# Modulation tiles of the first feed-forward network: three buffers of their own instead of the weights' raw buffers

## The chip, the cores and the metric

The kernel is one program on one NeuronCore of a Trainium2 chip. Its time is the device time of one execution in microseconds (us). The engines are named as in the profile: PE (TensorE, matrix products), PEld (its weight loads), DVE (VectorE), ACT (ScalarE), POOL (GpSimd) and SP (SyncE, which issues nearly all transfers). Each engine works through its own instructions in a fixed order.

## The reference

Two layers of a hybrid block run over 512 latent tokens and 256 context tokens of width 1024. Each layer has a token mixer (a state-space scan with heads, differential attention and an S5 scan side by side) and a convolutional feed-forward network of width 2816. Before and after each of them stand RMS norms, and shifts, scales and gates ("modulation") that are computed from a conditioning vector. The lines of the reference that matter here:

```python
mod_l = (jax.nn.silu(c) @ mod_w[layer] + mod_b[layer])[:, None, :]
mod_c = jax.nn.silu(c_ctx) @ mod_w[layer] + mod_b[layer]
sh_a, sc_a, g_a, sh_f, sc_f, g_f = jnp.split(mod_l, N_MOD, axis=-1)
...
def conv_ffn(h, w_gate, w_up, conv_w, conv_b, w_down):
    g = dwconv(h @ w_gate, conv_w, conv_b)
    return (jax.nn.silu(g) * (h @ w_up)) @ w_down
```

All of it is in float32. mod_w of one layer is a matrix of 1024 x 6144; the kernel has it as 48 tiles of 128 x 1024 (six groups j of eight tiles). The second layer's last group of context values isn't needed.

## The kernel before

**Products in float32.** A weight tile (128 x 1024, 512 KB) is loaded into a buffer with the tag "raw" (load_split, L129 to L139). ACT rounds it to a high half `hi` (L138), DVE subtracts that from the raw tile and writes the low half `lo` (L139). PE then makes three products for each tile: hi by hi, hi by lo and lo by hi (mm3, L144 to L146). There are two raw buffers (`w_raw` = 2) and three pairs of hi and lo (`w_hl` = 3).

**The first feed-forward network** (ffn, L1223) stands in the first layer, over 512 latent columns (products into pl) and 256 context columns (into pc). For each of the 22 slices f of the width of 2816 it loads wg, projects, applies the convolution on ACT and DVE (L1257, L1261), the silu (L1262), loads wu, projects, multiplies (L1267), and splits the result into ahi and alo (L1270, L1271). For each two slices the down projection (out_group, L1189) loads two wd tiles, makes the products into ma and adds them to y in SBUF: by ACT copies for the first pair (L1215), by DVE additions for the others (L1217). That is 66 weights in the whole network.

**Work put in between.** After each half of a slice `between()` (L1515) takes one or two steps of a generator `mod` and some of a generator `setup`. `setup` prepares the S5 scan of the second layer: small operations on DVE (L373 to L525), tables s5x on POOL (L551 to L556 and L598 to L603), products of those on PE (L568, L569) and transposes (L575). `mod` (L339) computes the modulation values: in this network mod_rest (L1569) has 56 tiles of mod_w left, eight of the first layer (j = 5) and all 48 of the second. Each tile is loaded by SP (L348); DVE multiplies it by a row (silu of c, "crow") and sums (L351). Where the context needs a value too (nv == 2: the first 24 of the 56 tiles), POOL multiplies the tile by the second row in place (L355) and ACT sums it (L357). The other 32 tiles have only L351.

**What sets the order.** The Python code gives the order in which work is declared; a scheduler then simulates times and orders each engine's instructions by them. A tile may be loaded into a buffer only when all who read its last contents are done. A pool's tag with bufs=n is a ring of n such buffers. In the kernel before, the 56 tiles take their buffers from the weights' ring: `raw=True` makes them the tag "raw" of the pool `self.W`, with `w_raw` = 2. SP issues all these loads in one queue, so a load that waits for its buffer holds back those behind it.

Of the kernel before, what the change touches and what calls it, by code (L numbers as in the profile page):

```python
# [92 lines left out]
class Kern:  # L93
# [242 lines left out]
                nc.vector.tensor_mul(o, o, wb)  # L336
                self.gate_out(l, j, nv)

    def mod(self, l, js, pool, row, pool_share, raw=False, pin=False):  # L339


        nc = self.nc
        for j in js:
            nv = 2 if l < L - 1 or j < 2 else 1
            for i in range(8):
                m = j * 8 + i
                w = self.t(self.W, [128, 1024], "raw", bufs=self.w_raw) if raw else self.t(pool, [128, 1024], "modw", bufs=2)
                nc.sync.dma_start(w, self.I["modw"][l, m])  # L348
                o = self.modc[l][:, m]
                jk = self.t(pool, [128, 1024], "modj", BF16, bufs=1)  # L350
                ins = nc.vector.scalar_tensor_tensor(jk, w, 1.0, row[:, 0], op0=ALU.mult, op1=ALU.mult, accum_out=o[:, 0:1])  # L351
                if pin:
                    self.tc.keep_in_program_order(ins)
                if nv == 2 and pool_share(i):
                    nc.gpsimd.tensor_mul(w, w, row[:, 1])  # L355
                    junk = self.t(self.small, [128, 1024], "junk", BF16, bufs=1)
                    nc.scalar.activation(junk, w, AF.Copy, accum_out=o[:, 1:2])  # L357
                elif nv == 2:
                    jk = self.t(pool, [128, 1024], "modj", BF16, bufs=1)
                    nc.vector.scalar_tensor_tensor(jk, w, 1.0, row[:, 1], op0=ALU.mult, op1=ALU.mult, accum_out=o[:, 1:2])  # L360
                if i < 7:
                    yield
            o = self.modc[l][:, j * 8:(j + 1) * 8, :nv]
            nc.vector.tensor_add(o, o, self.modb[:, l, j * 8:(j + 1) * 8, None].to_broadcast([128, 8, nv]))
            self.mod_scale(l, j, nv)
            yield
# [914 lines left out]
    def run(self):  # L1281
        tc, nc, I = self.tc, self.nc, self.I
        from contextlib import ExitStack
        with ExitStack() as es:
# [54 lines left out]
            M = self.modc[0]  # L1339
            mod = self.mod_pe((1, 0), PA)  # L1340
            pump(mod, 2)
            self.s5_disc(0, P0)
            v, g = nc.vector, nc.gpsimd
            setup = self.s5_setup(0, P0, (g, v, g, v, g, v, g, v), 2, True)
            pump(mod, 4)
            for t, nme in ((cst, "cst"), (self.nw, "nw"), (self.modb, "modb")):
                nc.sync.dma_start(t, I[nme])
            pump(setup, SU0)
            xts = []
            for t in range(6):  # L1350
                if t < 3:
                    pump(mod, 1)
                xt = self.t(PA, [128, 1024], "xr", bufs=6)
                nc.sync.dma_start(xt, xin(t))
                xts.append(self.normalise(xt, xt))
# [212 lines left out]

    def mod_rest(self, pool):  # L1569
        row = self.silu_rows(pool)  # L1570
        yield from self.mod(0, (5,), pool, row, lambda i: True, True)
        yield from self.mod(1, range(6), pool, row, lambda i: True, True)

    def open(self, name, bufs, kw):

# [148 lines left out]
```

## Time and profile before

| | |
|---|---|
| median of three runs | 1914.52 us (1913.77 to 1920.86) |
| profiled execution, its own time | 1921.23 us |
| its span, mean granted clock of PE | 1919.5 us, 0.957 |
| PE busy | 1736.8 us (90%) |
| DVE busy | 1258.9 us (66%) |
| ACT busy | 737.6 us (38%) |
| POOL busy | 541.3 us (28%) |
| transfers | 254.39 MB, 133 GB/s in the mean |

The busy time of an engine is the sum over its instructions; register, branch, semaphore and transfer-issuing instructions don't count. The first feed-forward network lies between about 560 and 1160 us of the span, the second between about 1560 and 1880. A row of a timeline gives the start, the duration, the engine, the line and what it writes and reads, and in brackets how long the engine had been idle and what ended it. A row of waits gives who waited, for whom, how long in sum, how often and the longest one.

### The profile page before, as it was taken

How to read it: one execution, taken by the hardware profiler on the slowest of the kernel's cores; microseconds unless marked ns; L12 is line 12 of the kernel's file. 1: busy time of each engine (PE TensorE's matmuls, PEld its weight loads, DVE VectorE, ACT ScalarE, POOL GpSimd, SP SyncE). 2: the span in 40 equal slices, each digit the busy share in tenths (PEclk: the TensorE clock that was granted, in tenths of full speed). 3: DMA queues.
4: the chain of work that ended last, by engine and by line, in shares of the span. 5: the costliest groups of instructions: out<-in, count | busy, mean ns of one | idle time of the engine just before them, and what ended most of it. 6: DMA issues, size and time to landing. Idle time of an engine off the chain costs nothing.

```text
span 1919.5 us, 25989 instructions
## 1 busy us (share of the span) xinstructions
PE 1736.8 (90%) x9573; PEld 1474.9 (77%) x9573; DVE 1258.9 (66%) x2201; ACT 737.6 (38%) x1383; POOL 541.3 (28%) x669
## 2 busy tenths in 40 slices
PE   6999787886999899999999997997888989999998
PEld 1788676775788788888778886885778788888886
DVE  6888997776568455556556557669667464555555
ACT  2443223755444433322122235533555444232322
POOL 5446940020235554412500024098000210000002
PEclk8999887998999999999999998998999999999999
DMA  8364347364443334434533433433285343232322
GB/s 313 133 198 144 121 143 202 89 182 119 168 133 99 104 117 132 135 129 128 168 121 126 146 107 120 133 111 113 88 204 117 132 157 112 83 110 79 119 77 88
DMA packets 128814, 254.39 MB, mean 133 GB/s; under 512 B 42608, under 2 KB 65712, under 8 KB 128688
## 3 DMA queue, kind: packets, MB, share of 16 engines
q1 hardware_dynamic: 125312, 249.57, 41.9%
q10 hardware_dynamic: 3376, 3.17, 0.5%
q8 instruction: 75, 1.23, 0.3%
q14 instruction: 51, 0.42, 0.1%
HBM read 213.53 MB, written 41.16 MB: 133 GB/s over the span
## 4 chain that ended last, share of the span: by engine, by line
PE 47%; DMA 11%; DVE 10%; POOL 4%; ACT 4%; issue 4%; SPq 1%; POOLq 0%; DVEq 0%; ACTq 0%
DMA raw<-in_modw 4%; PE pl L146 4%; PE pl L144 4%; PE pl L145 4%; PE ma L144 3%; PE ma L145 3%; PE ma L146 3%; PE pc L145 3%; PE pc L146 3%; PE pc L144 3%; DVE lo L139 3%; PE pp L144 3%; PE pp L145 3%; PE pp L146 3%; PE ma L1153 2%
## 5 line engine op out<-in xcount | busy, mean ns | idle before, releaser
L139 DVE TENSOR_TENSOR lo<-raw,hi 128x1024 fp32r<-128x1024 f32 (+2 forms) x190 | 248.3, 1310 | 191.6 <-ACT hi L138 190.4
L138 ACT CAST hi<-raw 128x1024 fp32r<-128x1024 f32 (+2 forms) x190 | 197.3, 1042 | 444.7 <-PE pl L145 128.1
L176 POOL TENSOR_SCALAR rv<-ss 128x1 f32<-128x1 f32 x51 | 20.6, 404 | 760.2 <-ACT junk L184 751.0
L146 PE MATMUL pl<-Hl,lo 128*128 128x512 f32 (+1 forms) x560 | 215.8, 385 | 12.8 <-DVE lo L139 12.8
L144 PE MATMUL pl<-Hl,hi 128*128 128x512 f32 (+1 forms) x560 | 215.5, 385 | 5.5 <-DVE xt L245 5.0
L145 PE MATMUL pl<-Hl,hi 128*128 128x512 f32 (+1 forms) x560 | 214.0, 382 | 0.0
L1217 DVE TENSOR_TENSOR y<-y,ma 128x512 f32<-128x512 f32 x160 | 106.6, 683 | 86.9 <-PE ma L146 86.7
L144 PE MATMUL ma<-hi,ahi 128*128 128x512 f32 x360 | 141.3, 393 | 5.9 <-DVE y L1217 5.9
L145 PE MATMUL ma<-lo,ahi 128*128 128x512 f32 x360 | 140.7, 391 | 0.1
L146 PE MATMUL ma<-hi,alo 128*128 128x512 f32 x360 | 139.8, 389 | 0.0
L351 DVE SCALAR_TENSOR_TENSOR modj<-raw,crow 128x1024 bf16<-128x1024 f32 x56 | 71.4, 1275 | 97.9 <-DMA raw<-in_modw 95.1
L146 PEld LDWEIGHTS pl<-Hl,lo 128*128 128x128 f32 x560 | 107.6, 192 | 33.9 <-DVE lo L139 14.7
L144 PEld LDWEIGHTS pl<-Hl,hi 128*128 128x128 f32 x560 | 107.7, 192 | 24.6 <-issue 5.2
L145 PEld LDWEIGHTS pl<-Hl,hi 128*128 128x128 f32 x560 | 107.3, 192 | 18.6
L144 PE MATMUL pp<-Hl,hi 128*128 128x512 f32 (+1 forms) x256 | 99.7, 392 | 13.4 <-DVE y L1217 5.5
L146 PE MATMUL pp<-Hl,lo 128*128 128x512 f32 (+1 forms) x256 | 98.1, 384 | 2.8 <-DVE lo L139 2.8
L144 PE MATMUL pc<-Hc,hi 128*128 128x256 f32 x352 | 99.6, 284 | 0.7 <-DVE de L394 0.7
L145 PE MATMUL pc<-Hc,hi 128*128 128x256 f32 x352 | 100.0, 284 | 0.2 <-DVE Hc L216 0.2
L146 PE MATMUL pc<-Hc,lo 128*128 128x256 f32 x352 | 99.7, 284 | 0.0
L145 PE MATMUL pp<-Hl,hi 128*128 128x512 f32 (+1 forms) x256 | 99.2, 388 | 0.2
L144 PE MATMUL pp<-hi,Hl 128*128 128x256 f32 (+1 forms) x256 | 89.3, 353 | 6.4 <-DVE xt L249 4.8
L145 PE MATMUL pp<-lo,Hl 128*128 128x256 f32 (+1 forms) x256 | 88.9, 347 | 2.4 <-DVE lo L139 2.4
(489 smaller groups left out, 4647.3 us busy)
## 6 DMA issues: line engine op xcount, KB each, us to landing
raw<-in_modw SPq DMA_DIRECT2D x56, 512.0 KB
raw<-in_wg SPq DMA_DIRECT2D x44, 512.0 KB
raw<-in_wu SPq DMA_DIRECT2D x44, 512.0 KB
raw<-in_wd SPq DMA_DIRECT2D x44, 512.0 KB
raw<-in_winf SPq DMA_DIRECT2D x28, 512.0 KB
modw<-in_modw SPq DMA_DIRECT2D x24, 512.0 KB
modw<-in_modwn SPq DMA_DIRECT2D x16, 512.0 KB
raw<-in_wout SPq DMA_DIRECT2D x16, 512.0 KB
```

The lines of the kernel that those rows point to most:

```text
L138: nc.scalar.copy(hi[:, :cols], raw[:, :cols])
L139: (eng or nc.vector).tensor_sub(lo[:, :cols], raw[:, :cols], hi[:, :cols].bitcast(F32))
L144: mm(out, lhs[0], rhs[0], start=first, stop=False)
L145: mm(out, lhs[0], rhs[1], start=False, stop=False)
L146: mm(out, lhs[1], rhs[0], start=False, stop=last)
L176: self.nc.gpsimd.tensor_scalar(v, ss, scale, eps, op0=ALU.mult, op1=ALU.add)
L351: ins = nc.vector.scalar_tensor_tensor(jk, w, 1.0, row[:, 0], op0=ALU.mult, op1=ALU.mult, accum_out=o[:, 0:1])
L1153: nc.tensor.matmul(o, wT[:, j * 128:(j + 1) * 128], v[:, kt * 128:(kt + 1) * 128], start=j == 0, stop=j == nk - 1)
L1217: nc.vector.tensor_add(y[:, t, c], y[:, t, c], pb[h])
```

## The change

The parameter `raw` of `mod` goes, and `bufs` takes its place. The 56 tiles of the first feed-forward network now come from their own pool M1 with the tag "modw" and three buffers. The weights keep the two buffers of "raw" for themselves. The other calls of `mod` keep two buffers as before. The pool M1 takes 12 KB more in each partition.

```diff
-    def mod(self, l, js, pool, row, pool_share, raw=False, pin=False):
+    def mod(self, l, js, pool, row, pool_share, bufs=2, pin=False):
...
-                w = self.t(self.W, [128, 1024], "raw", bufs=self.w_raw) if raw else self.t(pool, [128, 1024], "modw", bufs=2)
+                w = self.t(pool, [128, 1024], "modw", bufs=bufs)
...
-        yield from self.mod(0, (5,), pool, row, lambda i: True, True)
-        yield from self.mod(1, range(6), pool, row, lambda i: True, True)
+        yield from self.mod(0, (5,), pool, row, lambda i: True, 3)
+        yield from self.mod(1, range(6), pool, row, lambda i: True, 3)
```

The scheduler orders each engine anew. On POOL, before, the rows at the first table s5x of the S5 preparation (s5x_6289, L600); raw_6440 is the fourth modulation tile.

```order
L355 TENSOR_TENSOR raw_6440<-raw_6440,crow_6049 128x1024
L552 TENSOR_TENSOR s5b2g_6282<-s5bc_6278,s5cf_6060 128x32
L553 TENSOR_TENSOR s5bbg_6280<-s5a2g_6281,s5b2g_6282 128x32
L554 TENSOR_TENSOR s5a2g_6281<-s5bc_6278,s5cf_6060 128x32
L555 TENSOR_TENSOR s5b2g_6282<-s5bc_6278,s5cf_6060 128x32
L556 TENSOR_TENSOR s5bbg_6280<-s5a2g_6281,s5b2g_6282 128x32
L551 TENSOR_TENSOR s5a2g_6448<-s5bc_6278,s5cf_6060 128x32
L552 TENSOR_TENSOR s5b2g_6449<-s5bc_6278,s5cf_6060 128x32
L598 TENSOR_TENSOR stag_6290<-s5bbg_6280,s5ex_6061 128x256
L599 TENSOR_TENSOR stbg_6291<-s5bbg_6280,s5ex_6061 128x256
L600 TENSOR_TENSOR s5x_6289<-stag_6290,stbg_6291 128x2x128
L601 TENSOR_TENSOR stag_6290<-s5bbg_6280,s5ex_6061 128x256
```


After, the rows that end at the same L600; modw_7795 is the 22nd modulation tile, modw_7893 the 24th.

```order
L355 TENSOR_TENSOR modw_7795<-modw_7795,crow_6049 128x1024
L556 TENSOR_TENSOR s5bbg_6280<-s5a2g_6281,s5b2g_6282 128x32
L598 TENSOR_TENSOR stag_6290<-s5bbg_6280,s5ex_6061 128x256
L551 TENSOR_TENSOR s5a2g_6448<-s5bc_6278,s5cf_6060 128x32
L552 TENSOR_TENSOR s5b2g_6449<-s5bc_6278,s5cf_6060 128x32
L355 TENSOR_TENSOR modw_7886<-modw_7886,crow_6049 128x1024
L355 TENSOR_TENSOR modw_7893<-modw_7893,crow_6049 128x1024
L599 TENSOR_TENSOR stbg_6291<-s5bbg_6280,s5ex_6061 128x256
L676 TENSOR_TENSOR s5t_11222<-s5A_113 128x32
L678 TENSOR_TENSOR s5t_11222<-s5A_113 128x16
L600 TENSOR_TENSOR s5x_6289<-stag_6290,stbg_6291 128x2x128
L601 TENSOR_TENSOR stag_6290<-s5bbg_6280,s5ex_6061 128x256
```


All 24 L355 stand ahead of this L600 now, four did before.

On DVE, before, the rows that end at lo_6849 and lo_6932, the low halves of the fifth slice's wu and the sixth slice's wg; modj_6910 is the tenth modulation tile.

```order
L139 TENSOR_TENSOR lo_6739<-raw_6736,hi_6738 128x1024
L1271 TENSOR_TENSOR alo_6618<-g_6523,ahi_6617 128x768
L364 TENSOR_TENSOR modc_110<-modc_110,modb 128x16
L336 TENSOR_TENSOR modc_110<-modc_110,nw 128x16
L351 SCALAR_TENSOR_TENSOR modj_6821,modc_111<-raw_6819,crow_6049 128x1024
L351 SCALAR_TENSOR_TENSOR modj_6910,modc_111<-raw_6908,crow_6049 128x1024
L1261 SCALAR_TENSOR_TENSOR g_6792<-pl_6742,fcw,g_6792 128x511 x2
L139 TENSOR_TENSOR lo_6849<-raw_6846,hi_6848 128x1024
L139 TENSOR_TENSOR lo_6932<-raw_6929,hi_6931 128x1024
```


After, the rows that end at the same two; modj_8246 is the 28th modulation tile, modj_8685 the 34th.

```order
L351 SCALAR_TENSOR_TENSOR modj_8246,modc_111<-modw_8244,crow_6049 128x1024
L1261 SCALAR_TENSOR_TENSOR g_6792<-pl_6742,fcw,g_6792 128x511
L351 SCALAR_TENSOR_TENSOR modj_8328,modc_111<-modw_8326,crow_6049 128x1024
L351 SCALAR_TENSOR_TENSOR modj_8332,modc_111<-modw_8330,crow_6049 128x1024
L351 SCALAR_TENSOR_TENSOR modj_8398,modc_111<-modw_8396,crow_6049 128x1024
L351 SCALAR_TENSOR_TENSOR modj_8594,modc_111<-modw_8592,crow_6049 128x1024
L364 TENSOR_TENSOR modc_111<-modc_111,modb 128x8
L351 SCALAR_TENSOR_TENSOR modj_8605,modc_111<-modw_8603,crow_6049 128x1024
L336 TENSOR_TENSOR modc_111<-modc_111,nw 128x8
L139 TENSOR_TENSOR lo_6849<-raw_6846,hi_6848 128x1024
L351 SCALAR_TENSOR_TENSOR modj_8685,modc_111<-modw_8683,crow_6049 128x1024
L139 TENSOR_TENSOR lo_6932<-raw_6929,hi_6931 128x1024
```


Ahead of lo_6849 there are 33 L351 now, ten before; lo_6739, the low half of the fifth slice's wg, stands behind 22 instead of eight, and the low halves of the first two wd tiles behind 17 and 19 instead of seven. On PE, L568 with s5x_6289 stood between the wg and wu products of the fourth slice and now stands in the middle of the first down projection. On SP the last of the 56 loads now stands ahead of the 20th of the 66 weights; five loads of rows for the norm after the network stand ahead of one late weight.

## Rows read from the trace of the kernel before

**Rows 1.** Windows: length, busy us of PE, PEld, DVE, ACT, POOL; clock, DMA share, GB/s.
```profile
560.00:669.00 109.00, 97.32 (x550) 85.96 (x550) 74.52 (x209) 45.95 (x76) 53.68 (x64) 0.95 0.34 108
669.00:720.00 51.00, 49.56 (x269) 42.55 (x268) 30.73 (x40) 18.84 (x30) 24.18 (x20) 1.00 0.37 120
720.00:1158.00 438.00, 424.14 (x2235) 362.37 (x2233) 258.38 (x363) 120.21 (x163) 109.79 (x123) 1.00 0.42 134
1560.00:1880.00 320.00, 320.00 (x1464) 267.16 (x1464) 168.22 (x206) 106.10 (x130) 0.00 (x0) 1.00 0.30 94
```

**Rows 2.** PE waits, 560 to 669 us: what PE waited for, us, times, longest.
```profile
PE pl L146 <- DVE lo L139: 4.0, 1, 4.0
```

**Rows 3.** PE waits, 669 to 1158 us.
```profile
PE pl L146 <- DVE lo L139: 8.8, 6, 4.6
PE ma L144 <- DVE y L1217: 5.9, 6, 1.9
```

**Rows 4.** Waits of the SP queue, 500 to 1150 us.
```profile
SPq L348 <- DVE lo L139: 113.6, 28, 14.3
...
SPq L134 <- ACT junk L357: 77.8, 12, 9.7
```

**Rows 5.** Chain of waits, 660 to 690 us: start, us, what ran.
```profile
669.20 3.54 DMA raw<-in_modw
672.76 1.25 DVE modj L351 x2
...
674.13 2.42 POOL raw L355
676.57 1.16 ACT junk L357 x2
...
677.85 2.41 POOL raw L355
```

**Rows 6.** Timelines of PE at 622.6 and 669.2 us: start, us, line, operation.
```profile
622.65 0.30 PE L568 MATMUL mb<-s5bc,s5x 128*128 128x32 f32 x2
...
669.22 0.50 PE L146 MATMUL pl<-Hl,lo 128*128 128x512 f32 x1
```

**Rows 7.** Instruction counts by line, 555 to 1160 us: duration ns min/median/max, first and last start.
```profile
L139 DVE TENSOR_TENSOR lo<-raw,hi x64: 1215/1225/3403, 580.8 to 1124.8; 128x1024 fp32r<-128x1024 f32 x64
...
L351 DVE SCALAR_TENSOR_TENSOR modj<-raw,crow x56: 1209/1225/1982, 562.2 to 1071.2; 128x1024 bf16<-128x1024 f32 x56
...
L1271 DVE TENSOR_TENSOR alo<-g,ahi x22: 946/954/3158, 593.5 to 1126.0; 128x768 fp32r<-128x768 f32 x22
...
L355 POOL TENSOR_TENSOR raw<-raw,crow x24: 2348/2404/3472, 564.2 to 790.8; 128x1024 f32<-128x1024 f32 x24
```

**Rows 8.** Timeline of DVE, pieces from 556 to 629 us.
```profile
556.18 0.69 DVE L216 TENSOR_TENSOR Hl<-h,Hl 128x512 fp32r<-128x512 f32 x1
...
562.18 1.23 DVE L351 SCALAR_TENSOR_TENSOR modj<-raw,crow 128x1024 bf16<-128x1024 f32 x1 [2.36 <-DMA crow<-crd]
...
563.34 0.75 DVE L193 TENSOR_SCALAR xt<-xr,rr 128x1024 f32<-128x1024 f32 x1
564.27 2.35 DVE L394 TENSOR_SCALAR de<-s5prm 128x16 f32<-128x16 f32 x1 [0.19 <-DMA s5prm<-in_s5p]
...
587.14 0.17 DVE L427 TENSOR_SCALAR dscv<-dscv 128x16 f32<-128x16 f32 x1
587.22 0.68 DVE L1267 TENSOR_TENSOR g<-g,pl 128x512 f32<-128x512 f32 x1
...
628.72 3.40 DVE L139 TENSOR_TENSOR lo<-raw,hi 128x1024 fp32r<-128x1024 f32 x1 [2.59 <-ACT hi L138]
```

**Rows 9.** Timeline of POOL beside them.
```profile
564.22 2.37 POOL L355 TENSOR_TENSOR raw<-raw,crow 128x1024 f32<-128x1024 f32 x1 [2.93 <-DMA s5bc<-in_s5bk]
...
587.19 2.41 POOL L355 TENSOR_TENSOR raw<-raw,crow 128x1024 f32<-128x1024 f32 x1 [19.64 <-DVE de L401]
...
628.69 2.35 POOL L355 TENSOR_TENSOR raw<-raw,crow 128x1024 f32<-128x1024 f32 x1
```


## The prediction

> **What bounds the kernel now.** I read the busy shares first, then the stretches of the first feed-forward network, then PE's and SP's waits in them, then single instructions on DVE and POOL. In the windows [rows 1] PE is busy 97.3 of 109.0 us from 560 to 669, 49.6 of 51.0 up to 720 and 424.1 of 438.0 up to 1158, against 320.0 of 320.0 in the second network, where no modulation tile is loaded. So PE is the bound, and the first network leaves it idle for 11.7 + 1.4 + 13.9 = 27.0 us. That is the most the change can give back, apart from a slower pitch around each wait.
>
> What PE waits for is mostly the lo half of a weight (one wait of 4.0 us before 669, six with 8.8 us after), then y with 5.9 us [rows 2, 3]. Behind that stands the shared ring of two raw buffers: the SP queue holds a weight's load back for 77.8 us in sum because ACT has not yet read the modulation tile in the buffer, and a modulation load for 113.6 us until lo has been made [rows 4]. The chain of waits shows one round of such a tile: 3.54 us of load, 1.25 on DVE (L351), 2.42 on POOL (L355), 1.16 on ACT, 8.65 us from 669.20 to the next start at 677.85 [rows 5]. The change cuts this tie, and the PE waits behind it should go.
>
> **The change, part by part.** It removes no instruction and adds none. The 56 tiles get three buffers outside the ring, and the scheduler then pulls them forward: the excerpts of the order show all 24 POOL multiplies ahead of the first s5x (L600) of the network, where only 4 stood before, and lo_6849, the lo of the fifth slice's wu, behind the 33rd L351 instead of behind the 10th. All 24 tiles with two columns must therefore pass DVE and POOL before PE's L568, which now stands in the middle of the first down projection. Before, L568 ran at 622.65 without a wait [rows 6].
>
> The price lies in DVE and POOL. A DVE operation on SBUF operands and a POOL multiply do not run at the same time in this trace. L139 started at 628.72, 0.03 us after L355 at 628.69, and took 3.40 us against a median of 1.225 over 64; even the one-input L394, 16 columns wide (such operations take 0.17 us), took 2.35 us beside an L355 of 2.37; and the longest L355, 3.47 us against a median of 2.404, shows that POOL waits as well [rows 7 to 9]. L1267, which has an operand in PSUM, took its usual 0.68 at 587.22 beside that same kind of L355 (587.19 to 589.6). So SBUF work of the two engines adds up, and PSUM work of DVE does not.
>
> The sum for the stretch up to the first s5x (DVE rows up to the 24th L351, POOL rows up to L600):
> - DVE: 24 L351 x 1.225 = 29.4; 8 L139 x 1.225 = 9.8; 4 L1271 x 0.954 = 3.8; 8 L215 and L216 x 0.69 = 5.5; 2 L193 x 0.75 = 1.5; 127 small ones at 0.08, the distance from the start at 587.14 to the next at 587.22, = 10.2. Together 60.2 [rows 7, 8].
> - POOL: 24 L355 x 2.404 = 57.7, and some 12 small ones that I take at 5.
> - Sum 123 us. It can't begin before the first L351, which waits for crow and starts at 562.18 [rows 8]. So s5x is there at about 685 to 686.
>
> PE wants it much earlier. L568's new place is, by the order, 53 products (9.4 us at 97.32 us / 550 = 0.177 us each [rows 1]) ahead of the first product with lo_6849, which ran at 669.22 [rows 6]; so before, PE was at that place at 659.8, and without the waits that fall it would be there at about 651. It has to wait some 35 us, in pieces: at the lo halves of the two wd and of the next wg weight, which stand behind tiles 17, 19 and 22 on DVE, and at L568.
>
> Behind this, lo_6849 stands on DVE behind nine more tiles (25 to 33). They need no POOL; three buffers and 3.54 + 1.25 us give 1.6 us each, 14.4, and about 4 for the four s5A transfers that stand between them on SP: from about 684 to 703, plus 1.2 for lo itself. PE's first product with lo_6849 falls at about 704 instead of 669.2: **35 us later**. Queued behind the waiting instructions are, on DVE, wg's lo and the convolution of g, and on ACT the y copies of the first down projection, which now stand behind L357 of tiles 20 to 24; PE needs all of these, so nothing hides the 35.
>
> From there on the tiles cost nothing on PE's path: the last stands before the 20th of the 66 weights on SP, and the ring holds weights alone. The 13.9 us of idle time after 720 and the 1.4 ahead of it go, with some 2 of slow pitch around them: 17.3. I leave 3 for waits that come in their place (late in the network five row loads of the post-norm now stand ahead of a weight's load on SP), so about 14 come back. 35 - 14 = 21, of which I take **20 us**.
>
> These terms are from the profiled execution, 1921.23 us with a span of 1919.5, which lies 6.7 above the median of 1914.52 and within the three runs shown. I carry the difference, not the level: 1914.5 + 20 = **1935 us**, +1.0%.
>
> Bounds of the unknown. How well DVE and POOL pack when every tile needs both is not shown by a stretch of this kind. Without the small operations and the casts, of which no row shows that each stands aside for POOL, it is 13 us less, 110, and the change costs 7; with all of 17.3 given back and nothing in its place, 4. No clash at all is rival 1, a gain of 24. In the other direction: at 677.85 POOL's next multiply began only after ACT had read the last tile, 3.72 us after the one before [rows 5]; kept up over 24 tiles this leaves 24 x 1.31 = 31 us of gaps. DVE's tile operation of 1.23 fits such a gap when it is ready; if half the gaps stay empty the sum grows by 16 to +36, if all do, by 31 to +51. I stay at +20, nearest the rows for the single instructions, and keep -24 and +51 as ends.
>
> The Trainium skill (SBUF — State Buffer, section "SBUF: two separate sides") says that VectorE and GpSimd share one port pair, held as an exclusive lock for a whole instruction, and on VectorE's side only by an operation with two SBUF inputs or in a two-port mode. The rows on L139, L355 and L1267 agree. By its wording part of the one-input casts and small operations, some 9 us of the sum, would stay outside, and the forecast would be +11; the 2.35 us of L394 speak for leaving them in.
>
> **Rivals.**
> 1. *Faster: the tie is cut and the tiles run ahead unnoticed.* Without a clash POOL needs 57.7 + 5 = 63 us and is done at 625, before PE's 651. Three rounds of 8.65 us in flight give 2.9 us per tile, 24 tiles in 69 us, done at 631. PE then loses at most 3 of its 27 us again: 1914.5 - 24 = 1890. For it: the waits that the ring causes are real [rows 2 to 4]. Against it: rows 7 to 9, where the two engines exclude each other each time they meet. It wins where the joint sum is under 89 us (562 to 651).
> 2. *No change: costs and gains cancel.* If the joint sum is 10 to 15% smaller, 105 to 111, lo_6849 comes at 686 to 692, 17 to 23 us late, and 14 to 17 come back: 1915 to 1923. For it: the 13 us of small operations and casts above. Against it: L394, which is one of them [rows 8].
> 3. *Much slower: the gaps.* Half or more of the 1.31 us gaps stay empty because DVE, which takes its instructions in order, stands at a lo or a g that waits for ACT or PE while a tile is ready. Price 16 to 31 us above the forecast: 1951 to 1966. It decides once the mean distance of the 24 multiplies is over 5.8 us (my sum gives 123 / 24 = 5.1).
>
> That tiles don't move is no rival: the order shows that they do. A rule of the Trainium skill (Trainium Kernel Development and Optimization, section "Best Practices") speaks for rival 1: double-buffer, to overlap transfers with compute. By that rule alone the time would be that of rival 1; no row here shows a modulation tile in flight beside a free DVE and POOL.
>
> **How the numbers follow.** The forecast (1925 to 1950) has 0.50, rival 1 0.13, rival 2 0.17, rival 3 0.20. The range from 1907 to 1962 leaves out rival 1 and the top of rival 3, 0.19 in all; the forecast's own range is 1925 to 1950. A difference of under 0.5%, 9.6 us, can hardly be told from none here: faster 0.13, within 0.5% 0.17, slower 0.70.
>
> **What would show it.** Right: the 24 L355 start between 562 and 690 almost one behind another with mean distances of about 5 us; mean L139 and L351 in that stretch clearly above 1.225; PE idle for 30 us or more between 630 and 705, waiting for lo (L139), y or s5x; the first product with the fifth wu weight at about 704; from 760 to 1158 hardly any wait of PE. Wrong: the 24th L355 before 650, or DVE operations at 1.225 beside POOL's, which gives rival 1; multiplies 5.8 us or more apart with both engines idle between them, which gives rival 3; or new waits of PE after 760 of over 5 us, which would mean that the part given back is mis-sized.

## The result, and the profile after

The changed kernel takes 1940.1 us (median of four runs, 1936.34 to 1945.7) against 1914.14 us before (four runs, 1912.08 to 1920.86): a ratio of 1.0131, 95% interval [1.0111, 1.0151]. It is slower by 26 us by the medians; 1935 was forecast, in a range from 1907 to 1962. The profiled execution took 1936.34 us, with a span of 1934.5, so the two profiles lie only 15 us apart. A second profile of each kernel (below) accounts for a good half of that difference.

The windows of the changed kernel, with the columns of [rows 1]:

```profile
560.00:669.00 109.00, 80.47 (x431) 69.79 (x429) 106.33 (x214) 47.12 (x78) 57.68 (x30) 0.87 0.46 158
669.00:720.00 51.00, 43.24 (x208) 36.23 (x209) 46.36 (x71) 19.54 (x35) 49.28 (x46) 0.87 0.74 247
720.00:1158.00 438.00, 437.45 (x2336) 377.64 (x2336) 228.52 (x313) 109.81 (x141) 80.96 (x121) 1.00 0.31 100
```

PE has lost 16.9 us of busy time in the first window against [rows 1] and 6.3 in the second, its granted clock there fell from 0.95 and 1.00 to 0.87 (a part of the time at 1.2 instead of 2.4 GHz: 0.50 from 670 to 675 and from 700 to 705, behind waits shown below, against 1.00 from 595 to 625, where it had none), and DVE is busy for 106.3 of 109.0 us (74.5 before; standing beside POOL counts as busy) and POOL for 49.3 of the next 51.0 (24.2 before). Beside the 23.2 us of lost busy time there is a slower pitch: the 639 products of the first two windows took 0.194 us of busy time each instead of 0.179, 9 us in sum. From 720 on PE idles for 0.6 us, where it idled for 13.9. So the loss and the part given back stand in one profile, in two stretches.

POOL's timeline of the changed kernel, around tiles 15 and 16 and at the end of the burst:

```profile
635.47 2.41 POOL L355 TENSOR_TENSOR modw<-modw,crow 128x1024 f32<-128x1024 f32 x1 [1.22 <-ACT junk L357]
639.11 2.40 POOL L355 TENSOR_TENSOR modw<-modw,crow 128x1024 f32<-128x1024 f32 x1 [1.22 <-ACT junk L357]
...
677.14 4.77 POOL L355 TENSOR_TENSOR modw<-modw,crow 128x1024 f32<-128x1024 f32 x2
...
684.04 0.74 POOL L600 TENSOR_TENSOR s5x<-stag,stbg 128x256 f32<-128x256 f32 x1
```

DVE's timeline beside the first two rows:

```profile
635.91 3.05 DVE L351 SCALAR_TENSOR_TENSOR modj<-modw,crow 128x1024 bf16<-128x1024 f32 x1
...
638.89 0.17 DVE L422 TENSOR_TENSOR dssv<-dssv,dsr 128x16 f32<-128x16 f32 x1
...
639.13 0.68 DVE L1267 TENSOR_TENSOR g<-g,pl 128x512 f32<-128x512 f32 x1
639.73 1.81 DVE L423 TENSOR_TENSOR dssv<-dssv,dsr 128x16 f32<-128x16 f32 x1
```

This is the clash of [rows 8, 9], now without a break. L351 at 635.91 begins 0.44 us after POOL's multiply at 635.47, takes 3.05 us instead of 1.225 and ends just before the next multiply starts, at 639.11; POOL has stood 1.22 us by then, the length of one L351 (the profile names an ACT event before it as the releaser). That gap is an order of data: the multiply writes its tile in place, so the tile's own L351 must have read it. 22 of the 24 multiplies start 0.09 to 0.14 us after the end of their own L351. Nearly every multiply thus waits for DVE, and DVE then stands beside the multiply. A 16-column operation, L423 at 639.73, takes 1.81 us beside that multiply (L422 just before it takes 0.17), and L1267 with its operand in PSUM takes its usual 0.68. The last row of POOL is the first s5x, at 684.04.

What PE waited for in the changed kernel, 550 to 720 us:

```profile
PE pl L146 <- DVE lo L139: 9.0, 2, 5.9
PE ma L145 <- DVE lo L139: 5.8, 1, 5.8
PE pc L144 <- DVE de3a L378: 5.5, 1, 5.5
PE pl L144 <- ACT hi L138: 4.2, 1, 4.2
PE pl L144 <- DVE dse L440: 3.8, 1, 3.8
PE pl L144 <- DVE de3a L378: 3.7, 1, 3.7
...
PE mb L569 <- POOL s5x L603: 0.6, 1, 0.6
```

Before, the one large wait for lo in this stretch was 4.0 us [rows 2]. Left out are the waits of the norm ahead of the network and one of 0.4 us. The rows shown are eight waits of 32.6 us together (9.0 + 5.8 + 5.5 + 4.2 + 3.8 + 3.7 + 0.6), and all but the last are for DVE or ACT. Names like de3a are only the last event before the wait ended. The product with Hc (the network's input for the context columns, split into halves) waited until 577.86 for the halves of Hc, which stood on DVE behind a small operation beside a multiply:

```profile
572.00 2.31 DVE L387 TENSOR_SCALAR de1b<-de 128x16 f32<-128x16 f32 x1
...
574.39 0.64 DVE L216 TENSOR_TENSOR Hc<-h,Hc 128x512 fp32r<-128x512 f32 x1
...
576.08 0.69 DVE L216 TENSOR_TENSOR Hc<-h,Hc 128x512 fp32r<-128x512 f32 x1
...
577.74 0.69 DVE L216 TENSOR_TENSOR Hc<-h,Hc 128x512 fp32r<-128x512 f32 x1
```

PE's product with lo_6849:

```profile
701.95 0.80 PE L146 MATMUL pl<-Hl,lo 128*128 128x512 f32 x1 [5.93 <-DVE lo L139]
```

### The profile page after: what moved, and what is told of

It reads as the page before. It is cut to its first block, busy times and chain, and to the rows that moved or that the text cites. A ratio compares the mean times of both kernels' runs of the same rounds, so it can differ in the third digit from the quotient of the medians.

```text
span 1934.5 us, 26004 instructions
## 1 busy us (share of the span) xinstructions
PE 1741.8 (90%) x9573; PEld 1479.5 (76%) x9573; DVE 1291.3 (67%) x2201; ACT 736.8 (38%) x1383; POOL 554.1 (29%) x669
## 4 chain that ended last, share of the span: by engine, by line
PE 57%; DVE 11%; DMA 5%; issue 3%; ACT 3%; POOL 2%; SPq 1%; DVEq 0%; POOLq 0%; ACTq 0%
PE pl L146 6%; PE pl L144 6%; PE pl L145 6%; PE ma L144 4%; PE ma L145 4%; PE ma L146 4%; PE pc L145 4%; PE pc L144 4%; PE pc L146 4%; PE pp L144 3%; PE pp L145 3%; PE pp L146 3%; DVE lo L139 2%; PE ma L1153 2%; DVE modj L351 1%
## 5 line engine op out<-in xcount | busy, mean ns | idle before, releaser
L139 DVE TENSOR_TENSOR lo<-raw,hi 128x1024 fp32r<-128x1024 f32 (+2 forms) x190 | 246.3, 1300 | 179.5 <-ACT hi L138 177.0
L351 DVE SCALAR_TENSOR_TENSOR modj<-modw,crow 128x1024 bf16<-128x1024 f32 x80 | 122.2, 1527 | 19.0 <-DMA modw<-in_modw 18.8
```

The source lines that it names most:

```text
L139: (eng or nc.vector).tensor_sub(lo[:, :cols], raw[:, :cols], hi[:, :cols].bitcast(F32))
```

## The experiments

Twelve runs were made (ten kernels, and both kernels once more), in three groups of four, each group on one chip with its own runs of the kernel before (medians 1915.68, 1915.34 and 1914.87 us). Theory A is that of the prediction: SBUF work of DVE and POOL's multiplies add up, and tiles pulled forward in a burst delay the weights' low halves. Every edit makes the scheduler order the kernel anew, so no run changes one thing alone.

**e1_no_mult.** The multiply is left out; with it the context's modulation values.

```diff
-                    nc.gpsimd.tensor_mul(w, w, row[:, 1])
+                    pass
```

> The changed kernel without POOL's 24 multiplies L355: ACT sums the unmultiplied tile, so the context's modulation values are left out. The order runs even further ahead: 41 of the 56 tiles stand before the low half of the fifth slice's wu (33 in the changed kernel, 10 before). Theory A (SBUF work of DVE and POOL's multiplies exclude each other): without the 57.7 us of POOL, DVE alone needs 60 + 14 us (14 for its operations on PSUM) for the first 24 tiles, done at about 636, and 17 more tiles at 1.6 us; the fifth wu's low half comes at about 665 instead of 702, the PE waits after 720 stay away, 1897 us (1890 to 1905). Theory B (the tiles ahead in DVE's and SP's queues cost by their place alone, POOL has no part in it): about the changed kernel's time, 1930 to 1950.

Measured: 1905.59 us, ratio 0.9946 [0.9927, 0.9964]. The tiles are as early as ever, even earlier, and the loss is gone: theory B falls. L351 and L139 are back at their bare times, and the product with lo_6849 runs at 670.59, against 665 expected, 701.95 in the changed kernel and 669.22 before:

```profile
L351 DVE SCALAR_TENSOR_TENSOR modj<-modw,crow 128x1024 bf16<-128x1024 f32 x48 | 58.4, 1217 | 10.6 <-DMA modw<-in_modw 10.4
L139 DVE TENSOR_TENSOR lo<-raw,hi 128x1024 fp32r<-128x1024 f32 x12 | 14.6, 1217 | 1.4 <-ACT hi L138 1.4
```

```profile
670.59 0.79 PE L146 MATMUL pl<-Hl,lo 128*128 128x512 f32 x1
```

The time is 8 us above the point that A gave, just outside its range (1905). PE is busy for 147.3 of the 160 us from 560 to 720, no more than before (146.9), so the burst still costs what PE's old waits there cost; only the part after 720 came back.

**e2_mult_on_dve.** The second product is made by DVE.

```diff
-        yield from self.mod(0, (5,), pool, row, lambda i: True, 3)
-        yield from self.mod(1, range(6), pool, row, lambda i: True, 3)
+        yield from self.mod(0, (5,), pool, row, lambda i: False, 3)
+        yield from self.mod(1, range(6), pool, row, lambda i: False, 3)
```

> The changed kernel with the second product of the 24 tiles on DVE (a second L351-like operation with its own sum) instead of POOL's L355 and ACT's L357; the result is complete. 23 tiles stand before the low half of the fifth wu. Theory A: 24 x 2.404 us of POOL become 24 x 1.225 of DVE, so the joint sum falls by 28 us; the fifth wu's low half comes at about 668 to 675 instead of 702; 1905 us (1897 to 1915). Theory B (DVE's queue alone): DVE gets 29 us more to do ahead of the same weights, slower than the changed kernel: 1950 to 1970.

Measured: 1902.27 us, 0.9930 [0.9905, 0.9956]. DVE got 24 operations more and the kernel became 38 us faster than the changed one, as only A has it. The product with lo_6849 runs at 663.97, a little ahead of the 668 to 675 expected. Groups by line on DVE from 562 to 690 us (count, busy us, mean ns, idle before). The changed kernel:

```profile
L351 DVE SCALAR_TENSOR_TENSOR modj<-modw,crow 128x1024 bf16<-128x1024 f32 x28 | 48.9, 1747 | 5.1 <-DMA modw<-in_modw 5.1
L139 DVE TENSOR_TENSOR lo<-raw,hi 128x1024 fp32r<-128x1024 f32 x8 | 11.9, 1494 | 0.0
```

The kernel with the multiply on DVE:

```profile
L351 DVE SCALAR_TENSOR_TENSOR modj<-modw,crow 128x1024 bf16<-128x1024 f32 x33 | 40.1, 1214 | 3.4 <-DMA modw<-in_modw 3.4
...
L139 DVE TENSOR_TENSOR lo<-raw,hi 128x1024 fp32r<-128x1024 f32 x13 | 15.8, 1216 | 1.4 <-ACT hi L138 1.4
```

Without POOL's multiplies L351 has its bare 1.214 us on average, over 33 of them, and L139 1.216; beside them it was 1.747 and 1.494. With e1's 1.217 for both, that is the clash measured by itself. (The first s5x comes at 690.02 in e1 and 697.68 in e2, with no multiply ahead of it; across kernels its time is no measure of the multiplies.)

**e3_one_buffer.** One own buffer instead of three (`lambda i: True, 1`).

> The changed kernel with one buffer of its own instead of three. A tile's round (load 3.54, DVE 1.25, POOL 2.42, ACT 1.16, 8.4 to 8.65 us in all) then limits the tiles to one each 8.65 us, and the order stays near that of before: 5 multiplies stand ahead of the first s5x (24 in the changed kernel, 4 before), 11 tiles ahead of the fifth wu's low half (33, 10). Theory A: the burst is gone, and so is the tie to the weights' ring; most of the 27 us of PE's idle time comes back: 1893 us (1888 to 1903). Rival C (the gain in the changed kernel came from the tiles being early, not from the ring being free): the tiles again meet the weights over the whole network, SP's queue stands at the one buffer, 1908 to 1920.

Measured: 1937.6 us, 1.0117 [1.0077, 1.0158], as slow as the changed kernel. Both expectations missed. There is no burst (order and POOL as before) and no shared ring, and still PE waits more than before. The waits of PE for lo and those of DVE for a tile, 555 to 1160 us; the kernel before:

```profile
PE pl L146 <- DVE lo L139: 12.8, 7, 4.6
DVE modj L351 <- DMA raw<-in_modw: 95.1, 42, 7.6
```

With one own buffer:

```profile
PE pl L146 <- DVE lo L139: 26.8, 12, 6.5
DVE modj L351 <- DMA modw<-in_modw: 115.2, 45, 8.7
```

DVE comes to an L351 whose tile has not landed and stands there, 95 us in sum before and 115 now, and the low halves of weights stand behind it. Where two tiles follow one another, the second can't be loaded until the first has been read. So waits for lo arise without a shared ring too, and the ring of the kernel before need not be the whole reason for its PE waits. That DVE's standing is what makes them is argued here; e9 and e10 test it.

**e4_pinned.** Three own buffers, and each L351 keeps its place in the program.

```diff
-        yield from self.mod(0, (5,), pool, row, lambda i: True, 3)
-        yield from self.mod(1, range(6), pool, row, lambda i: True, 3)
+        yield from self.mod(0, (5,), pool, row, lambda i: True, 3, True)
+        yield from self.mod(1, range(6), pool, row, lambda i: True, 3, True)
```

> The changed kernel, three own buffers, with each L351 kept in program order on DVE, so that the tiles can't be pulled forward: 1 multiply ahead of the first s5x, 7 tiles ahead of the fifth wu's low half. Theory A: no burst, no tie: 1893 us (1888 to 1903). Rival C as in the run with one buffer: 1908 to 1920, because DVE then stands at an L351 whose tile has not landed and the low halves wait behind it.

Measured: 1891.64 us, 0.9880 [0.9839, 0.9921], as A had it. In its trace DVE never waits for a modulation tile: the tile lands early and its L351 comes late. PE is busy for 154.0 of 160 us up to 720 and for 280.0 of 280.0 from 800 to 1080.

**e5_own_first24** and **e6_own_last32.** Own buffers for one part of the tiles; the others stay in the ring.

```diff
-                w = self.t(pool, [128, 1024], "modw", bufs=bufs)
+                w = self.t(self.W, [128, 1024], "raw", bufs=self.w_raw) if bufs == 3 and nv == 1 else self.t(pool, [128, 1024], "modw", bufs=bufs)
```

(and with `nv == 2` for e6).

> Own buffers for the first 24 tiles alone (those with POOL's multiply); the last 32 stay in the weights' ring as before. 24 multiplies stand ahead of the first s5x as in the changed kernel, but 24 tiles instead of 33 ahead of the fifth wu's low half. Theory A (the burst of tiles on DVE and POOL costs about 33 us, the freed ring gives back 14 to 18 after it): the burst stays, less the 9 tiles, some 20 to 25 us, and little is given back because 32 tiles still share the ring: 1934 us (1927 to 1942). Rival (the late tiles are the harm, by 32 transfers ahead of the weights): 1900 to 1912.

> Own buffers for the last 32 tiles alone (those without POOL); the first 24 stay in the weights' ring. Theory A: no burst of POOL's multiplies; the stretch up to 800 stays as before, the PE waits after it go (about 8 of the 13.9 us after 720), perhaps 2 to 4 us for a burst of ten tiles on DVE: 1907 us (1901 to 1912). Rival (the late tiles are the harm): 1930 to 1942.

Measured: 1938.84 us, 1.0112 [1.0088, 1.0136], for the first 24; 1914.66 us, 0.9993 [0.9978, 1.0007], for the last 32. The first 24 tiles alone bring the whole loss. The last 32 alone bring nothing, where 8 us were expected. Their L351 come 32 in a row from 791.8 to 871.5 and need 1.373 us on average, and PE idles for 3.7 us from 800 to 1080 instead of 10.9 in the first profile of before, but 6.7 in the second one: there was less to win than the first profile said. What it wins there it loses elsewhere: from 560 to 1158 PE idles for 22.9 us in it and for 22.6 in the second profile of before.

**e7_ring_pinned.** The kernel before with pinned L351 (`lambda i: True, True, True` in its two calls).

> The kernel before, all tiles in the weights' ring, but with each L351 kept in program order on DVE: 9 tiles ahead of the fifth wu's low half (10 before). It tells whether the pinned run was fast by its order alone. Theory A (own buffers give the gain where nothing is pulled forward): the ring still ties tiles and weights, 1914 us (1906 to 1922). Rival (the order alone gives it): 1890 to 1898.

Measured: 2117.38 us, 1.1046 [1.1020, 1.1072]. Both missed by 200 us. PE's waits, 555 to 1160 us:

```profile
PE pl L144 <- ACT hi L138: 116.1, 16, 12.1
```

and those of the SP queue (the window ends before this kernel's network does):

```profile
SPq L134 <- ACT junk L357: 100.8, 8, 24.1
SPq L134 <- DVE modj L351: 74.2, 5, 21.5
```

Here a tile that waits for its pinned place holds one of the two raw buffers, and weights go through the other. This is the tie of the ring at its strongest, and it says that pinning is worth something only with own buffers.

**e8_changed_again** and **e12_before_again.** Both kernels once more.

> The changed kernel once more, for a second profile and more runs of both kernels on one chip: 1938 us (1934 to 1944); first s5x (L600) within 3 us of 684, first product with the fifth wu's low half within 3 us of 702. If another profile puts the loss at another place than the stretch from 560 to 720, theory A has no case.

> The kernel before once more, for a second profile: the profiles of before and after lie 15 us apart, the medians 26. If the first profile of before was one of its slower executions, this one has a span of 1906 to 1914 and ends the first network about 5 to 8 us earlier; if not, the span is about 1919 again and the missing 10 us belong to no stretch that a profile shows. Time 1915 us (1908 to 1922).

Measured: 1939.18 us (ratio 1.0119 [1.0094, 1.0145]) and 1915.24 us (0.9998 [0.9979, 1.0017]). The first s5x came at 687.06 and the product with lo_6849 at 704.50 in the second profile of the changed kernel, 3.0 and 2.6 us later than in the first, as is its first L351 (565.6 against 562.6). The last additions to y of the first network, from counts by line: first profile of before, second profile of before, first and second of the changed kernel:

```profile
L1217 DVE TENSOR_TENSOR y<-y,pl x6: 675/685/689, 1131.8 to 1164.8; 128x512 f32<-128x512 f32 x6
```

```profile
L1217 DVE TENSOR_TENSOR y<-y,pl x6: 674/686/689, 1128.3 to 1161.2; 128x512 f32<-128x512 f32 x6
```

```profile
L1217 DVE TENSOR_TENSOR y<-y,pl x6: 676/685/689, 1146.3 to 1179.2; 128x512 f32<-128x512 f32 x6
```

```profile
L1217 DVE TENSOR_TENSOR y<-y,pl x6: 673/684/689, 1148.9 to 1181.8; 128x512 f32<-128x512 f32 x6
```

From the first L351 (562.2, 565.9, 562.6, 565.6) to the last of these the network takes 602.6 and 595.3 us before, 616.6 and 616.2 after. The network of the first profile of before was 7 us longer. The expectation for e12 was met in part: the network ended 3.6 us earlier by the clock of the span (its first L351 came 3.7 us later), and the span is 1916.3 us, neither the 1906 to 1914 nor the 1919 named. Against the second profile the change costs 20.9 us, by the profiled times (1918.09 and 1939.2) 21.1.

**e9_pinned_one**, **e10_pinned_two.** The pinned kernel with one and with two buffers.

> The pinned kernel with one buffer instead of three. In the run with one buffer and free order DVE stood 115 us at an L351 whose tile had not landed, with low halves of weights behind it; in the pinned run with three buffers it never did. Theory D (that standing is what makes PE wait once there is no burst): with one buffer the second of two tiles in a row comes 4.8 to 8.6 us after the first, DVE stands some 50 us or more in sum, the PE waits for lo come back: 1907 us (1899 to 1920). Rival A (only the burst and the ring matter, pinning removes the one and own buffers the other): 1892 us (1888 to 1897).

> The pinned kernel with two buffers. Theory D: two tiles in a row both find a buffer, DVE stands little (under 15 us), 1893 us (1889 to 1899). Rival (three are needed): 1900 to 1910.

Measured: 1925.01 us, 1.0047 [1.0028, 1.0066], with one; 1892.62, 0.9883 [0.9858, 0.9908], with two. Waits of PE for lo and of DVE for a tile, 555 to 1160 us, with one pinned buffer and then with two:

```profile
PE pl L146 <- DVE lo L139: 19.5, 12, 3.8
DVE modj L351 <- DMA modw<-in_modw: 87.3, 38, 7.4
```

```profile
PE pl L146 <- DVE lo L139: 0.2, 1, 0.2
DVE modj L351 <- DMA modw<-in_modw: 5.4, 5, 2.1
```

Theory D holds in kind: the standing of DVE comes back with one buffer and with it 19.5 us of PE's waits for lo. The price was sized too low, 33 us against three buffers instead of 15, and the time lies above D's range (1920). The SP queue, too, stands for the one buffer, with weights behind it; no run separates that from DVE's standing. Against it speaks that DVE waits less for a weight's high half with one buffer (38.6 us) than with two (69.5).

**e11_pinned_dve.** Pinned, three buffers, the second product on DVE (`lambda i: False, 3, True`).

> The pinned kernel with three buffers and the second product of the 24 tiles on DVE instead of POOL and ACT; complete result. A try at a faster one. Theory A: the pinned kernel's PE idles some 6 us between 560 and 720; half of it may go as L139 and L351 fall back to 1.22 us: 1889 us (1885 to 1894). Rival (DVE's 29 us more are in the way of low halves and of g): 1894 to 1900.

Measured: 1885.03 us, 0.9839 [0.9807, 0.9871], the fastest of all, with the whole result. PE is busy for 157.8 of 160 us from 560 to 720.

| kernel | us | multiplies on POOL ahead of the first s5x | DVE standing at L351 for its tile, us |
|---|---|---|---|
| before | 1914.87 | 4 | 95.1 |
| changed | 1940.1 | 24 | 10.9 |
| e1, no multiply | 1905.59 | none | 10.4 |
| e2, multiply on DVE | 1902.27 | none | 5.4 |
| e3, one buffer | 1937.6 | 5 | 115.2 |
| e5, own buffers for the first 24 | 1938.84 | 24 | 55.0 |
| e6, own buffers for the last 32 | 1914.66 | 6 | 44.9 |
| e9, pinned, one buffer | 1925.01 | 0 | 87.3 |
| e10, pinned, two buffers | 1892.62 | 0 | 5.4 |
| e4, pinned, three buffers | 1891.64 | 1 | none |
| e11, pinned, multiply on DVE | 1885.03 | none | none |

The kernels clearly faster than before (e1, e2, e4, e10, e11) have neither the burst of POOL's multiplies nor more than 11 us of a DVE that stands. The last column is not a price list: e6 has less than half the standing of the kernel before and the same time, e9 has a little less and is 10 us slower. e7 is left out; it has neither (1.9 us of standing) and is the slowest, by the ring.

## Why the prediction was right

**The joint sum of DVE and POOL.** Forecast: 123 us from the first L351, the first s5x at 685 to 686. Measured: from 562.6 to 684.04, 121.4 us, and 565.6 to 687.06, 121.5, in the second profile. e1 and e2 show the cause: without POOL's multiplies the operations of DVE have their bare times and the loss is gone. In the changed kernel DVE is busy for all of this stretch:

```profile
562.58:684.04 121.46, 121.33 (x238) 0.86 0.45 150
```

So no transfer and no buffer was the limit there; DVE was. That the sum came within 2 us is partly luck, as two of its terms were off against each other. In the timeline of the stretch each of the 24 multiplies has one operation of DVE standing beside it until it is over, 1.6 to 2.2 us longer than such an operation takes alone, some 48 us in sum: POOL cost DVE that much, and not the 62.7 us of the forecast. DVE's operations on PSUM, which the forecast left out as running beside POOL, took 15.5 us, and only 5.7 of that fell beside the multiplies. What remains, some 57 us of SBUF work, is near the forecast's 60. The Trainium skill (SBUF — State Buffer, section "SBUF: two separate sides") calls the shared port pair an exclusive lock for a whole instruction; the 3.05 us of L351 agree (it ends 1.08 us after the multiply beside it). The forecast's estimate that some 9 us of one-input operations might stay outside is not borne out for L387, a one-input TENSOR_SCALAR, which took 2.31 us; for the casts the sum can't tell.

**The delay at lo_6849.** Forecast: 35 us, at 704. Measured: 701.95, that is 139.4 us after the first L351, against 107.0 in the profile before (32.4 later) and 104.2 in the second one (34.7 later).

**Where PE waits.** This part was half right, and one of the forecast's signs was missed: PE idles for 19.6 us between 630 and 705, not for 30 or more. L568 was to be the place that waits for the 24 multiplies; PE waited only 0.6 us there for s5x. It had been held up before: 13.0 us at three products of the first network's early projections (Hc and the first weights, 5.5, 3.7 and 3.8), which were not named, then 5.8 at a wd's lo, 4.2 and 3.0 at the next wg and 5.9 at lo_6849, which were. Part of the delay was not waiting at all but the slower pitch of 9 us. Since DVE was the bound, it made no difference to the sum where PE stood.

**What comes back.** Forecast: 14 of 17.3 us. Measured, from the product with lo_6849 to the last addition to y: 495.6 us before, 477.3 after, 18.3 against the profile that the forecast was made from; 491.1 and 13.8 against the second one. PE's waits from 720 to 1158 fell to 0.6 us. Runs in which the tiles end early agree: from 872 to 1080 PE idles for 0.4 us in e1, e6 and the changed kernel, 7.5 and 3.9 in the two profiles of before, and 7.2 in e5, whose late tiles share the ring. The late row loads, for which 3 us were left, cost nothing that shows.

**The carry to the median.** The forecast took +20 from the profile. The first pair of profiles gives +14 to +15, the second +21, the medians +24 to +26. The forecast places its profile (1921.23 us) within the three runs shown; it lies just above the highest, 1920.86. That profile of before held a network 7 us longer than its second one: so its 32.4 us late less 18.3 given back make 14.1, while 34.7 less 13.8 in the second one make 20.9, near the forecast's 35 and 14. The last 3 to 5 us between profiles and medians lie within the spread of the runs and have no place in a profile.

**What was wrong in the reasons.** The prediction read PE's old waits as the ring's doing alone. e3 and e9 show the same waits without any shared ring, and e10 against e9 that they go where DVE no longer stands at an L351 for a late tile. Of the rivals, the first (1890, tiles ahead and hidden) is what the pinned kernels are: 1891.64 and 1892.62. In the changed kernel it failed by the clash: e1 and e2, which have the early tiles without POOL's multiplies, come to 1905.59 and 1902.27.

What stays open: why e3 is 12 us slower than e9, with much the same standing of DVE (115 and 87 us); and how much of the 38 us between the changed kernel and e2 is DVE's standing beside POOL and how much the lighter order of DVE and ACT that came with it (23 tiles ahead of lo_6849 instead of 33). Why e9, with a little less standing of DVE than the kernel before, is 10 us slower than it is open too. The multiply on POOL in a place where DVE has only PSUM work was not tried.

## What to carry to other kernels

A buffer more lets a scheduler pull side work forward, and then the work's own price shows: add up what the engines that hold each other up (here DVE and POOL, in their SBUF work) must do in the stretch into which it moves, and compare with the bound engine's time there. Own buffers paid here with a fixed order of the side work (e4, e10, e11) or without POOL's multiplies (e1, e2); and an operation should come up in its queue after its data has landed, since everything behind it waits too. Check a sum that fits term by term, since errors can cancel. Take a second profile of the kernel before, where the effect is near the spread of its runs.

## What the runs showed of the hardware

Each multiply of the burst held up one DVE operation on SBUF until it was over, however short that operation was: a 16-column one of 0.17 us took 1.81 us beside a multiply (L423), another 2.31 (L387, one input), and the 128x1024 L351 3.05. In proportion the small ones pay most. Such one-input and 16-column operations had been left open in the forecast's lower bound. POOL can be the one that stands: the L139 that started at 630.81, 0.03 us after a multiply, kept its 1.21 us, and that multiply took 3.47 instead of 2.40. An operation with an operand in PSUM did not stand (L1267, 0.68). Pinning the order without own buffers cost 10.5% (e7), far more than any other edit.
